# Recording a three-part product as three operations, and letting the scheduler place a wide product between two transposes

## The chip, the core and the metric

The kernel runs on one core of a Trainium2 chip. The metric is the device time of one execution in microseconds (us); the runs shown give the median of 3. The core's engines have queues of their own that run in order: TensorE (PE; its weight loads are a row of their own, PEld), VectorE (DVE), ScalarE (ACT), GpSimd (POOL), SyncE (SP, which issues transfers). A row of the trace names engine, source line, operation, and "written<-read" tiles by kind: s in SBUF, p and a in PSUM, m small tiles.

## The reference

Two decoder layers on 512 tokens of width 1024. Each mixes tokens by two attentions on one input projection (one with an index that selects 128 keys, one "stick-breaking"), gates and merges them, and then runs a mixture of 16 experts of which each token uses two. Cut to what matters:

```python
for l in range(DEPTH):
    proj = x @ w_in[l]                        # q, k, v, index, gates
    y_a = dsa_attention(...)                  # top-k by an indexer, softmax
    y_b = stick_breaking_attention(...)       # sigmoid, reversed cumulative product
    merged = g_a * (y_a @ w_branch_a) + g_b * (y_b @ w_branch_b)
    x = layer_norm(DN_ALPHA * x + merged @ w_out, ...)
    for e in range(N_EXPERTS):                # of the tokens whose combine[:, e] is not 0
        h = silu(xf @ exp_w_gate[e]) * (xf @ exp_w_up[e])
        y = y + combine[:, e:e + 1] * (h @ exp_w_down[e])
    x = layer_norm(DN_ALPHA * x + y, ...)
```

## The kernel before

**Products.** To keep float32 accuracy at the speed of the rounded type `float32r`, both factors are split into a high and a low part (`Chip.split`: a cast on ACT at L484, a subtraction on DVE at L495), and a product is three matmuls into one PSUM tile: low x high, high x low, high x high. `Chip.mm3` makes them. Most have a 128x128 stationary operand and 512 columns; I call one such matmul a wide product. There are about 5000 of them.

**Transposes.** Where a result has to be turned, PE transposes 128x128 pieces through the identity (`Chip.tr`, L445): 888 times. In the attentions they turn the probabilities of one head (1 to 4 pieces each), in the experts the gathered tokens (8 pieces for an expert, `prep`) and the hidden layer (4 pieces, `down`, function `turn`). I call them turns, as the change does.

**Order of the work.** The kernel is not written in the order in which it runs. Every call records an `Op` with an engine, an assumed duration and the buffers that it reads and writes. `Recorder.plan` then plays a list scheduler: at each step it takes the engine that is free first, and of the operations that are ready there the one with the lowest `prio` (the place in which it was recorded, moved by `bump`). A planned start sets nothing but the order: the instructions are issued engine by engine in that order, and the chip runs each queue in order, with semaphores between engines. What is planned too early therefore waits at the head of its queue, and holds what stands behind it. In the plan a turn takes 0.11 us, and a three-part product is one operation, so nothing can stand between its matmuls:

```python
        if transpose is not None:
            dur = 0.11
...
    def mm3(self, out, lh, ll, rh, rl, start, stop):
        return self.mm(out, [(ll, rh), (lh, rl), (lh, rh)], start, stop)
```

**Stages.** Per layer: projections, indexer, both attentions and the gates woven together (80 to 365 us in the first layer, 800 to 1130 in the second); the output projection and the router (to about 440 and 1205); the 16 experts (to about 745 and 1500); the second norm. An expert needs 6.3 MB of weights, read by SP in 512 KB pieces. The tokens of an expert are fetched by an indirect transfer that POOL issues (`gather`, L1179) into a tile that `prep` turns. That fetch also claims the two `xh` tiles into which the turned tokens are split, and these exist for three experts, so the fetch for expert e waits until PE has read the tokens of expert e-3 for the last time. Result rows are scattered by POOL at L1185. The first expert takes its tokens from PSUM, without a fetch.

Of the kernel before, what the change touches and what calls it, by code (L numbers as in the profile page):

```python
# [11 lines left out]
F = mybir.dt.float32  # L12
FR = mybir.dt.float32r
# [15 lines left out]
NE = 16  # L29
# [56 lines left out]

class Op:
    __slots__ = ("eng", "dur", "fn", "deps", "prio", "allocs", "bufs", "succ", "wait", "ready", "start", "end", "nbytes",
                 "table", "n", "load", "cnt", "cols")


class Recorder:
# [3 lines left out]
    LAT = 0.14  # L96

    def __init__(self, nc, tc):
        self.nc, self.tc, self.ops, self.bump, self.after = nc, tc, [], 0, None
        self.plain = bacc.Bacc("TRN2", target_bir_lowering=False, num_devices=1)  # L100
        self.shapes, self.masks, self.tokens = {}, {}, {}

# [19 lines left out]
            self.masks[key] = (m if p0 < 64 else 0) | ((m << 64) if p0 + n > 64 else 0)  # L122
        return self.masks[key]

    def add(self, eng, dur, fn, writes=(), reads=(), wtok=(), rtok=(), nbytes=0, table=None, allocs=(), load=None):
        o = Op()
        o.eng, o.dur, o.fn, o.nbytes, o.table = eng, dur, fn, nbytes, table
        o.prio = len(self.ops) - self.bump
        o.deps, o.allocs, o.succ, o.n = set(), [], [], len(self.ops)
        bufs = {}  # L130
        for vs, wr in ((reads, False), (writes, True)):
            for v in vs:
                if not isinstance(v, View):
                    continue
                b, m = v.buf, self.mask(v)
                if not b.hist and b.slot is None:
                    assert wr, "read before any write"
                for m2, w2, o2 in b.hist:
                    if (wr or w2) and m & m2:
                        o.deps.add(o2)  # L140
                bufs[b] = 1
        for vs, wr in ((reads, False), (writes, True)):
            for v in vs:
                if isinstance(v, View):
                    b, m = v.buf, self.mask(v)
                    if b.first is None:
                        b.first = (o.prio, o.n)
                    if wr:
                        b.hist = [h for h in b.hist if h[0] & ~m or h[2] is o]
                    b.hist.append((m, wr, o))  # L150
        for v in allocs:
            bufs[v.buf] = 1
            if v.buf.first is None:
                v.buf.first = (o.prio, o.n)
        for toks, wr in ((rtok, False), (wtok, True)):
            for t in toks:
                h = self.tokens.setdefault(t, [])
                for w2, o2 in h:
                    if (wr or w2) and o2 is not o:
                        o.deps.add(o2)  # L160
                if wr:
# [12 lines left out]

    def plan(self):
# [6 lines left out]
        ready = {e: [] for e in engs}  # L182
        barrier = []
        dma_free, hw_free = 0.0, 0.0
        table = None
        left = {}
        frees = []
        for o in self.ops:
# [96 lines left out]
        while done < len(self.ops):  # L285
# [16 lines left out]
            else:  # L302
# [7 lines left out]
                if e == "ACT" and table is not None:  # L310
                    keep = [x for x in ready[e] if x[2].table in (None, table)]
                    if keep:
                        x = min(keep)
                        if x[0] < ready[e][0][0] + 400:
                            ready[e].remove(x)
                            heapq.heapify(ready[e])
                            o = x[2]
                if o is None:
                    o = heapq.heappop(ready[e])[2]
                o.allocs = [b for b in o.bufs if b.slot is None]  # L320
# [39 lines left out]
            else:  # L360
                if e == "ACT" and o.table is not None and o.table != table:
                    table = o.table
                    dur += 1.3
                if e == "PE":
                    if busy.get(int(t / TICK) - 1, 0) < COLUMNS:
                        dur *= 2
                    k = int((t + dur) / TICK)
# [52 lines left out]
class Chip:  # L420
# [10 lines left out]
    def psum(*vs):  # L431
        return 0.06 if any(isinstance(v, View) and v.buf.kind in "pa" for v in vs) else 0.0

    def mm(self, out, terms, start, stop, transpose=None, also=()):
        dt = {F: 4, FR: 1, BF: 1}
        n = self.n(out)
        if transpose is not None:
            dur = 0.11
        else:
            dur = sum(max(dt[x.dtype if not isinstance(x, View) else x.ap.dtype] * n, 256) / 2400 + 0.004 for _, x in terms)  # L440

        def fn():
            o = real(out)
# [5 lines left out]
        o = self.r.add("PE", dur, fn, [out], reads, allocs=also)  # L449
        o.cols = sum(n * w.shape[0] / P for w, _ in terms) + n * (transpose is not None)  # L450
        o.cnt = sum(2 if (x.ap.dtype if isinstance(x, View) else x.dtype) == F else 1 for _, x in terms) + (transpose is not None)
        return o

    def mm3(self, out, lh, ll, rh, rl, start, stop):
        return self.mm(out, [(ll, rh), (lh, rl), (lh, rh)], start, stop)

    def mm_side(self, outs, terms, stop, also=()):

# [77 lines left out]
THROTTLE = 3  # L536
CAP0, CAP1, CAP2 = 12, 19, 29
BUMP, KEEP, LATE, NXT = 50, 1, 0, 3


QUOTA = {"raw": 3, "w": 6, "wi": 10, "wo": 12, "ew": 24, "at": 2, "pt": 6, "xg": 2, "xh": 6, "x": 46}
# [2 lines left out]
def build(tc, x0, xT0, w_idx, w_main, w_br, w_out, w_exp, bgate, idxg, idxb,  # L544
          ln1g, ln1b, ln2g, ln2b, wrt, rbias, ln1c, hconst, tab0, out):
    nc = tc.nc
    with ExitStack() as ctx:
# [703 lines left out]
        def moe(l, tb, gi, gl, mci, loads, xacc, until, routed):  # L1251
# [24 lines left out]
            def gate_up(e, xhl, between=None):  # L1276
                xh, xl = xhl
                for i in (0, 2):
# [4 lines left out]
                    for c in parts:  # L1283
                        for kk in range(KD):
# [1 line left out]
                                w += weights(e, i + kk // 4)  # L1286
                            o = C.mm3(ps[:, c], xh[:, kk, :], xl[:, kk, :], w[kk][0][:, c], w[kk][1][:, c], kk == 0, kk == KD - 1)
                            if done is not None:
                                o.deps.add(done)
                        done = o  # L1290
                        if i:
                            C.tt(sg[:, c], sg[:, c], ps[:, c], OP.mult)
# [318 lines left out]
```

## Time and profile before

| | |
|---|---|
| median of 3 runs | 1542.97 us (1541.4 to 1545.42) |
| the profiled execution | 1544.22 us, span 1542.5 us |
| mean granted clock of PE | 0.985 of 2.4 GHz |
| PE busy | 1477.8 us (96%) |
| DVE busy | 1268.0 us (82%) |
| ACT busy | 896.6 us (58%) |
| DMA | 313 MB; 325 GB/s in the experts' stages |

Busy time of PE is the union of its matmul rows, whose ends are modelled. What a matmul takes away from the next is read from the distance of two starts instead. The profiled execution is 1.25 us longer than the median of the runs; 1.7 us of it lie outside the span.

### The profile page before, as it was taken

What the parts mean: (1) busy time and instruction counts of PE and PEld (TensorE: products, weight loads), DVE (VectorE), ACT (ScalarE), POOL (GpSimd) and SP (SyncE); (2) the same over time, 40 slices, a digit from 0 to 9 for tenths busy, and PEclk for the clock granted to TensorE, in tenths of its full rate; (3) what the DMA queues carried; (4) which work ended last, traced back from release to release, by engine and by line L of the source; (5) the groups of instructions that cost most, each with busy time, mean ns of one, the idle gap of its engine ahead of it and who ended that gap; (6) DMA issues with size and microseconds to landing.
All of it is one profiled execution on the core that took longest, in us unless ns stands there. A gap on an engine that the chain in (4) does not pass through costs nothing. (4 is left out here: it accounts for less than half of the span.)

```text
span 1542.5 us, 21103 instructions
## 1 busy us (share of the span) xinstructions
PE 1477.8 (96%) x7188; PEld 1177.3 (76%) x7188; DVE 1268.0 (82%) x2321; ACT 896.6 (58%) x1459; POOL 128.4 (8%) x131
## 2 busy tenths in 40 slices
PE   8999999999989999999799999999999899999985
PEld 7877777777867788888487777777778578877874
DVE  5699995877687999989875999867766889899987
ACT  4335543674147888888433455346841578878773
POOL 0000000000131211111010000000001311111100
PEclk9999999999999999999899999999999899999998
DMA  7222113118778899999712211221287789999993
GB/s 222 72 84 67 57 55 96 56 42 304 268 249 307 328 349 343 335 337 332 297 69 67 85 55 55 83 82 55 68 316 254 260 309 337 347 331 323 351 328 147
DMA packets 92708, 313.15 MB, mean 203 GB/s; under 512 B 15757, under 2 KB 15885, under 8 KB 92592
## 3 DMA queue, kind: packets, MB, share of 16 engines
q1 hardware_dynamic: 83152, 294.88, 54.6%
q0 software_dynamic: 9440, 16.83, 3.0%
q8 instruction: 60, 0.98, 0.3%
q14 instruction: 56, 0.46, 0.1%
HBM read 302.19 MB, written 25.31 MB: 212 GB/s over the span
## 5 line engine op out<-in xcount | busy, mean ns | idle before, releaser
L447 PE MATMUL p<-s,s 128*128 128x512 f32 (+1 forms) x5192 | 1267.1, 397 | 30.0 <-DVE s L495 25.0
L447 PEld LDWEIGHTS p<-s,s 128*128 128x128 f32 x5192 | 950.2, 190 | 240.2 <-DVE s L495 25.6
L495 DVE TENSOR_TENSOR s<-s,s 128x1024 fp32r<-128x1024 f32 (+3 forms) x534 | 621.2, 1196 | 140.2 <-ACT s L484 106.8
L484 ACT CAST s<-s 128x1024 fp32r<-128x1024 f32 (+2 forms) x526 | 515.7, 1030 | 200.9 <-PE p L447 130.6
L495 DVE TENSOR_TENSOR s<-a,s 128x256 fp32r<-128x256 f32 (+3 forms) x386 | 168.8, 480 | 43.9 <-ACT s L484 40.4
L484 ACT CAST s<-a 128x256 fp32r<-128x256 f32 (+2 forms) x354 | 126.2, 414 | 123.7 <-PE a L445 107.1
L445 PE MATMUL a<-ident,s 128*128 128x128 f32 x888 | 132.3, 277 | 12.4 <-DMA s<-x1d,m 7.1
L445 PEld LDWEIGHTS a<-ident,s 128*128 128x128 f32 x888 | 106.2, 142 | 43.6 <-DVE s L495 11.4
L523 POOL TENSOR_TENSOR m<-m,nhalf 128x1 f32<-128x1 f32 x24 | 17.8, 743 | 902.1 <-DVE m L495 902.1
L480 ACT ACTIVATE s<-a 128x512 f32<-128x512 f32 (+3 forms) x156 | 61.8, 450 | 47.1 <-PE a L447 28.0
L484 ACT COPY s<-a 64x512 f32<-64x512 f32 (+1 forms) x48 | 27.8, 583 | 97.2 <-PE a L445 45.9
L487 ACT ACTIVATE s<-p,m 128x512 f32<-128x512 f32 (+1 forms) x64 | 44.2, 690 | 53.5 <-PE p L447 49.3
L464 PE MATMUL a<-s,s 64*128 64x384 f32 (+3 forms) x456 | 67.4, 351 | 0.0
L1179 POOL DMA_INDIRECT s<-x1d,m x30 | 42.9, 1430 | 265.6 <-PE p L447 248.3
L1185 POOL DMA_INDIRECT yd<-s,m x32 | 46.1, 1440 | 209.6 <-ACT s L487 189.6
L447 PEld LDWEIGHTS a<-s,s 128*128 128x128 f32 x360 | 57.1, 188 | 7.8 <-issue 2.4
L447 PE MATMUL a<-s,s 128*128 128x324 f32 (+4 forms) x360 | 62.4, 321 | 0.2
L464 PEld LDWEIGHTS a<-s,s 64*128 64x128 f32 x456 | 41.3, 185 | 27.6 <-issue 20.0
L495 DVE MAX8 m<-s 128x8 f32<-128x256 f32 (+2 forms) x96 | 53.5, 557 | 1.8
L495 DVE MATCH_REPLACE8 s<-m,s 128x256 f32<-128x256 f32 (+2 forms) x96 | 52.1, 543 | 0.0
L495 DVE TENSOR_TENSOR_SCAN s<-s 128x128 f32<-128x128 f32 (+3 forms) x64 | 51.1, 814 | 0.1
L484 ACT CAST s<-p 128x512 fp32r<-128x512 f32 x48 | 27.9, 588 | 35.6 <-DVE p L495 19.8
(108 smaller groups left out, 650.6 us busy)
## 6 DMA issues: line engine op xcount, KB each, us to landing
s<-in_w_exp SPq DMA_DIRECT2D x384, 512.0 KB
s<-in_w_main SPq DMA_DIRECT2D x79, 512.0 KB
s<-in_w_br SPq DMA_DIRECT2D x16, 512.0 KB
s<-in_w_out SPq DMA_DIRECT2D x16, 512.0 KB
s<-yd SPq DMA_DIRECT2D x16, 512.0 KB
x1d<-s SPq DMA_DIRECT2D x8, 512.0 KB
s<-x1d SPq DMA_DIRECT2D x8, 512.0 KB
s<-in_w_idx SPq DMA_DIRECT2D x8, 324.0 KB
```

The source lines that it names most:

```text
L445: self.nc.tensor.transpose(o, real(transpose[0]), transpose[1])
L447: self.nc.tensor.matmul(o, real(w), real(x), start=start and i == 0, stop=stop and i == len(terms) - 1)
L464: self.nc.tensor.matmul(real(o), real(t[i][0]), real(t[i][1]), start=i == 0, stop=stop and i == len(t) - 1)
L480: self.nc.scalar.activation(real(out), real(src), func, bias=real(bias), scale=real(scale), **kw)
L484: return self.r.add("ACT", 0.1 + self.psum(out, src) + self.n(out) * 0.833e-3, lambda: self.nc.scalar.copy(real(out), real(src)), [out], [ ...
L487: return self.r.add("ACT", 0.2 + self.n(out) * 0.833e-3, lambda: self.nc.scalar.mul(real(out), real(src), real(c)), [out], [src, c])
L495: getattr(self.nc.vector, method)(real(out), *[real(a) for a in args], **{k: real(x) for k, x in kw.items()}, **({} if accum is None else ...
L523: return self.r.add("POOL", 0.47, lambda: self.nc.gpsimd.tensor_tensor(real(out), real(a), e, OP.pow), [out], [a])
L1179: R.add("POOL", 1.04, lambda: nc.gpsimd.indirect_dma_start(out=real(dst), out_offset=None, in_=x1d, in_offset=IOA(ap=real(idx), axis=0), * ...
L1185: s_ = nc.gpsimd.indirect_dma_start(out=yd, out_offset=IOA(ap=real(idx), axis=0), in_=real(src), in_offset=None, bounds_check=2 * S - 1, o ...
```

## The change

Three edits. `mm3` records its three matmuls as three operations; the first two are marked `more`, so that the count from which `prio` is taken (`tick`) goes on only once per product. Operations on PE get a `form`: "turn" for a transpose or a narrow float32 product, "wide" for a `float32r` product with 256 columns or more. And in `plan`, when the last operation on PE was a turn and the next by priority is a turn too, the first ready wide one whose `prio` is less than 1000 behind is taken ahead of it. A turn that follows something other than a turn is planned 0.075 us shorter. In the experts' `gate_up` the order between the two halves of the last product now binds all three operations.

```diff
@@ class Recorder: add
-        o.prio = len(self.ops) - self.bump
+        o.prio, o.form = self.tick - self.bump, form
+        self.tick += not more
...
@@ plan
+                if e == "PE" and form == "turn" and ready[e][0][2].form == "turn":
+                    for x in sorted(x for x in ready[e] if x[2].form == "wide" and x[0] < ready[e][0][0] + NEAR):
+                        x[2].allocs = [b for b in x[2].bufs if b.slot is None]
+                        if x[2].allocs:
...
+                            w = room(x[2], t)
+                            if w is None or w > t + 1e-9:
+                                continue
+                        ready[e].remove(x)
+                        heapq.heapify(ready[e])
+                        o = x[2]
+                        break
...
                 if e == "PE":
+                    if o.form == "turn" and form != "turn":
+                        dur -= 0.075
+                    form = o.form
...
@@ class Chip: mm
+        form = None
+        if transpose is not None or n <= 2 * NE and kinds == [F]:
+            form = "turn"
+        elif n >= 256 and kinds[0] == FR:
+            form = "wide"
...
     def mm3(self, out, lh, ll, rh, rl, start, stop):
-        return self.mm(out, [(ll, rh), (lh, rl), (lh, rh)], start, stop)
+        self.mm(out, [(ll, rh)], start, False, more=True)
+        self.mm(out, [(lh, rl)], False, False, more=True)
+        return self.mm(out, [(lh, rh)], False, stop)
...
+NEAR = 1000
...
@@ gate_up
                             if done is not None:
-                                o.deps.add(done)
+                                for x in R.ops[-3:]:
+                                    x.deps.add(done)
```

The same matmuls are issued, 888 turns and all products among them. What moves is their order, and with it the order on the other engines. Counted over the whole program, 698 turns were followed directly by a turn and 180 are now; of the 518 pairs that are parted, 174 lie in the experts (85 and 89 in the two layers), 344 elsewhere. Turns that stand alone between two other matmuls go from 28 to 654.

**Place 1: PE in an attention of the first layer.** Two heads' probabilities (s_2918 before, s_2831 after, three pieces each, into two PSUM tiles a) are turned beside a projection into four p tiles. Before:

```order
L445 MATMUL a_2971<-ident,s_2918 128x128 x3
L447 MATMUL p_2658<-s_195,s_2696 128x512
L447 MATMUL p_2658<-s_212,s_2663 128x512
L447 MATMUL p_2658<-s_195,s_2663 128x512
L447 MATMUL p_2675<-s_195,s_2696 128x512
L447 MATMUL p_2675<-s_212,s_2663 128x512
L447 MATMUL p_2675<-s_195,s_2663 128x512
L445 MATMUL a_2992<-ident,s_2918 128x128 x3
L447 MATMUL p_2692<-s_195,s_2696 128x512
L447 MATMUL p_2692<-s_212,s_2663 128x512
L447 MATMUL p_2692<-s_195,s_2663 128x512
```

The turns stand in two runs of three, and whole three-part products between the runs. Now, the same turns on the same engine:

```order
L463 MATMUL a_2911<-ident,s_2831 128x128
L465 MATMUL p_2861<-s_137,s_2733 128x512
L463 MATMUL a_2911<-ident,s_2831 128x128
L465 MATMUL p_2861<-s_139,s_2700 128x512
L463 MATMUL a_2911<-ident,s_2831 128x128
L465 MATMUL p_2861<-s_137,s_2700 128x512
L463 MATMUL a_2925<-ident,s_2831 128x128
L465 MATMUL p_2889<-s_137,s_2733 128x512
L463 MATMUL a_2925<-ident,s_2831 128x128
L465 MATMUL p_2889<-s_139,s_2700 128x512
L463 MATMUL a_2925<-ident,s_2831 128x128
```

Each run of three turns is opened, and one matmul of a three-part product (into p_2861, then p_2889) stands behind each turn.

**Place 2: PE in the first layer's experts.** Before, the hidden layer of an expert (s_5780) and the tokens of expert 9 (s_5674, eight pieces) are turned in one run of twelve, between the gate product of expert 8 (p_5902) and its up product (p_5980):

```order
L447 MATMUL p_5902<-s_5924,s_5492 128x512
L447 MATMUL p_5902<-s_5914,s_5492 128x512
L447 MATMUL p_5902<-s_5914,s_5493 128x512
L447 MATMUL p_5902<-s_5924,s_5492 128x512
L447 MATMUL p_5902<-s_5914,s_5492 128x512
L445 MATMUL a_5955<-ident,s_5780 128x128 x4
L445 MATMUL a_5966<-ident,s_5674 128x128 x4
L445 MATMUL a_5971<-ident,s_5674 128x128 x4
L447 MATMUL p_5980<-s_5922,s_5493 128x512
L447 MATMUL p_5980<-s_5936,s_5492 128x512
L447 MATMUL p_5980<-s_5922,s_5492 128x512
```

Nothing stands between the twelve. Now the same pattern is found one expert later, for the tokens of expert 10 (s_5865) and the gate and up products of expert 9 (p_6083, p_6138):

```order
L465 MATMUL p_6083<-s_6105,s_5679 128x512
L465 MATMUL p_6083<-s_6093,s_5679 128x512
L463 MATMUL a_6136<-ident,s_5979 128x128
L465 MATMUL p_6138<-s_6102,s_5680 128x512
L463 MATMUL a_6136<-ident,s_5979 128x128
L465 MATMUL p_6138<-s_6116,s_5679 128x512
L463 MATMUL a_6136<-ident,s_5979 128x128
L465 MATMUL p_6138<-s_6102,s_5679 128x512
L463 MATMUL a_6136<-ident,s_5979 128x128
L465 MATMUL p_6138<-s_6102,s_5680 128x512
L463 MATMUL a_6154<-ident,s_5865 128x128
L465 MATMUL p_6138<-s_6116,s_5679 128x512
```

The run of twelve has become twelve single turns, with eleven wide products between them.

**Place 3: PE at the tokens of expert 9, now.** The activations of expert 6 (s_5122 high, s_5123 low) are read for the last time in the fifth row of this piece; from there on the fetch for expert 9 may start:

```order
L465 MATMUL p_5604<-s_5651,s_5122 128x512
L465 MATMUL p_5604<-s_5634,s_5122 128x512
L465 MATMUL p_5604<-s_5634,s_5123 128x512
L465 MATMUL p_5604<-s_5651,s_5122 128x512
L465 MATMUL p_5604<-s_5634,s_5122 128x512
L465 MATMUL p_5664<-s_5660,s_5510 128x512
L465 MATMUL p_5664<-s_5642,s_5510 128x512 x2
L465 MATMUL p_5664<-s_5660,s_5510 128x512
L465 MATMUL p_5664<-s_5642,s_5510 128x512
```

The rows after the fifth already belong to the down product of expert 5 (p_5664). Further on the first turn of the tokens of expert 9 (s_5678) stands here, in the fourth row, between two matmuls of the gate product of expert 7 (p_5735):

```order
L465 MATMUL p_5699<-s_5671,s_5510 128x512
L465 MATMUL p_5735<-s_5713,s_5304 128x512
L463 MATMUL a_5609<-ident,s_5479 128x128
L463 MATMUL a_5739<-ident,s_5678 128x128
L465 MATMUL p_5735<-s_5724,s_5303 128x512
L465 MATMUL p_5735<-s_5713,s_5303 128x512
L465 MATMUL p_5735<-s_5713,s_5304 128x512
L465 MATMUL p_5735<-s_5724,s_5303 128x512
L465 MATMUL p_5735<-s_5713,s_5303 128x512
```

Between the last reading and this turn stand 24 wide products and 5 turns. Before, the tokens of expert 9 were turned behind the gate product of expert 8 (place 2), 120 wide products and 16 turns after the same point. Now the distance is also short for expert 4 (24 products, 4 turns) and expert 14 (30, 5) of the first layer, and for expert 5 (19, 12), expert 10 (24, 5) and expert 15 (30, 5) of the second; for every other expert from the fourth on it is 37 products or more, and before it was 66 or more for all.

## Rows read from the trace of the kernel before

**Rows 1.** The page: busy time of PE, and its two large groups.
```profile
PE 1477.8 (96%) x7188; PEld 1177.3 (76%) x7188; DVE 1268.0 (82%) x2321; ACT 896.6 (58%) x1459; POOL 128.4 (8%) x131
...
L447 PE MATMUL p<-s,s 128*128 128x512 f32 (+1 forms) x5192 | 1267.1, 397 | 30.0 <-DVE s L495 25.0
...
L445 PE MATMUL a<-ident,s 128*128 128x128 f32 x888 | 132.3, 277 | 12.4 <-DMA s<-x1d,m 7.1
```

**Rows 2.** Windows: stretch, length, busy of PE, PEld, DVE, ACT, POOL, clock, DMA.
```profile
80.00:365.00 285.00, 283.15 (x1442) 219.86 (x1440) 240.16 (x546) 151.99 (x341) 0.00 (x0) 1.00 0.23 74
...
440.00:745.00 305.00, 292.01 (x1377) 238.01 (x1376) 272.38 (x290) 244.10 (x293) 52.83 (x39) 0.99 0.91 325
...
800.00:1130.00 330.00, 328.31 (x1659) 256.54 (x1657) 262.45 (x606) 165.51 (x362) 1.19 (x2) 1.00 0.22 71
...
1205.00:1500.00 295.00, 283.48 (x1307) 230.21 (x1305) 260.91 (x277) 233.61 (x280) 47.16 (x39) 0.99 0.92 325
```

**Rows 3.** Waits of PE in all: total, times, longest.
```profile
PE p L447 <- DVE s L495: 31.1, 27, 6.8
PE a L445 <- DMA s<-x1d,m: 7.1, 3, 2.7
```

**Rows 4.** Timeline, attention: start, length, engine, line, operation, count; single turns.
```profile
297.61 0.14 PEld L445 LDWEIGHTS a<-ident,s 128*128 128x128 f32 x1
297.84 0.27 PE L445 MATMUL a<-ident,s 128*128 128x128 f32 x1
297.84 0.54 PEld L447 LDWEIGHTS p<-s,s 128*128 128x128 f32 x3
297.87 0.94 PE L447 MATMUL p<-s,s 128*128 128x512 f32 x3
...
298.65 0.27 PE L445 MATMUL a<-ident,s 128*128 128x128 f32 x1
```

**Rows 5.** Timeline of PE, experts: fifteen wide products and the next turn.
```profile
1479.67 3.56 PE L447 MATMUL p<-s,s 128*128 128x512 f32 x15
1483.07 0.60 PE L445 MATMUL a<-ident,s 128*128 128x128 f32 x4
```

**Rows 6.** Timeline of PE, experts: runs of twelve turns.
```profile
563.38 1.47 PE L445 MATMUL a<-ident,s 128*128 128x128 f32 x12
564.61 16.62 PE L447 MATMUL p<-s,s 128*128 128x512 f32 x72
581.07 1.47 PE L445 MATMUL a<-ident,s 128*128 128x128 f32 x12
```

**Rows 7.** Timeline of PE, attention: a run of four.
```profile
907.40 0.60 PE L445 MATMUL a<-ident,s 128*128 128x128 f32 x4
907.76 2.31 PE L447 MATMUL p<-s,s 128*128 128x512 f32 x9
909.91 1.37 PE L447 MATMUL a<-s,s 128*128 128x512 f32 x8
```

**Rows 8.** Timeline of POOL: the fetch in the cycle of rows 6; line L1179's landing.
```profile
570.62 1.49 POOL L1179 DMA_INDIRECT s<-x1d,m  x1 [10.29 <-PE p L447]
...
DMA to landing us min/median/max: 4.5/7.2/9.1
```

**Rows 9.** Timeline of PE at the ends of both expert stages: last weights.
```profile
733.11 0.98 PE L447 MATMUL p<-s,s 128*128 128x256 f32 x6 [0.97 <-DVE s L495]
...
735.96 1.21 PE L447 MATMUL p<-s,s 128*128 128x256 f32 x8 [0.74 <-DVE s L495]
737.68 2.78 PE L447 MATMUL p<-s,s 128*128 128x256 f32 x21 [0.51 <-DVE s L495]
...
1501.86 4.95 PE L447 MATMUL p<-s,s 128*128 128x256 f32 x27 [4.53 <-PEq L1203]
```

More of the change, by code (lines that the diff above doesn't have):

```diff
@@ L88 @@
     __slots__ = ("eng", "dur", "fn", "deps", "prio", "allocs", "bufs", "succ", "wait", "ready", "start", "end", "nbytes",
-                 "table", "n", "load", "cnt", "cols")
+                 "table", "n", "load", "cnt", "cols", "form")
 class Recorder:
@@ L98, in __init__ @@
     def __init__(self, nc, tc):
-        self.nc, self.tc, self.ops, self.bump, self.after = nc, tc, [], 0, None
+        self.nc, self.tc, self.ops, self.bump, self.after, self.tick = nc, tc, [], 0, None, 0
         self.plain = bacc.Bacc("TRN2", target_bir_lowering=False, num_devices=1)
@@ L123, in mask, with add @@
         return self.masks[key]
-    def add(self, eng, dur, fn, writes=(), reads=(), wtok=(), rtok=(), nbytes=0, table=None, allocs=(), load=None):
+    def add(self, eng, dur, fn, writes=(), reads=(), wtok=(), rtok=(), nbytes=0, table=None, allocs=(), load=None, form=None, more=False):
         o = Op()
         o.eng, o.dur, o.fn, o.nbytes, o.table = eng, dur, fn, nbytes, table
-        o.prio = len(self.ops) - self.bump
+        o.prio, o.form = self.tick - self.bump, form
+        self.tick += not more
         o.deps, o.allocs, o.succ, o.n = set(), [], [], len(self.ops)
@@ L184, in plan @@
         dma_free, hw_free = 0.0, 0.0
-        table = None
+        table, form = None, None
         left = {}
@@ L317, in plan @@
                             o = x[2]
+                if e == "PE" and form == "turn" and ready[e][0][2].form == "turn":
+                    for x in sorted(x for x in ready[e] if x[2].form == "wide" and x[0] < ready[e][0][0] + NEAR):
+                        x[2].allocs = [b for b in x[2].bufs if b.slot is None]
+                        if x[2].allocs:
+                            for s in slots.values():
+                                s.sort()
+                            w = room(x[2], t)
[5 more added lines that the diff above has]
+                        break
                 if o is None:
@@ L432, in psum, with mm @@
         return 0.06 if any(isinstance(v, View) and v.buf.kind in "pa" for v in vs) else 0.0
-    def mm(self, out, terms, start, stop, transpose=None, also=()):
+    def mm(self, out, terms, start, stop, transpose=None, also=(), more=False):
         dt = {F: 4, FR: 1, BF: 1}
@@ L439, in mm @@
         else:
-            dur = sum(max(dt[x.dtype if not isinstance(x, View) else x.ap.dtype] * n, 256) / 2400 + 0.004 for _, x in terms)
+            kinds = [x.dtype if not isinstance(x, View) else x.ap.dtype for _, x in terms]
+            dur = sum(max(dt[k] * n, 256) / 2400 + 0.004 for k in kinds)
         def fn():
@@ L448, in mm @@
         reads = [x for t in terms for x in t] + ([transpose[0]] if transpose else [])
-        o = self.r.add("PE", dur, fn, [out], reads, allocs=also)
+        form = None
[3 more added lines that the diff above has]
+            form = "wide"
+        o = self.r.add("PE", dur, fn, [out], reads, allocs=also, form=form, more=more)
         o.cols = sum(n * w.shape[0] / P for w, _ in terms) + n * (transpose is not None)
```

## The prediction

> **What bounds the kernel now.** I read the page first, then busy time by stage, then single starts on PE. The page shows PE busy for 96% of the span, nearly all of it in the wide products and the turns [rows 1]. The windows show where that is a bound: in the two attention stretches PE is busy for 283.15 of 285 us and 328.31 of 330, at full clock [rows 2]. The waits of PE over the whole run come to about 40 us, 31.1 on DVE and 7.1 on the fetch of tokens [rows 3]; hardly any lie in the attentions. So there each 10 ns that a matmul takes more or less moves the end. In the expert stages PE is busy for 292 of 305 and 283 of 295 us, while the DMA engines are at 0.91 and 0.92 [rows 2]: two bounds close together, and at the end of both stages PE waits for the last weights, 0.97 + 0.74 + 0.51 = 2.2 us in the first layer and 4.5 in the second [rows 9].
>
> **What a turn costs, and whether a wide product beside it makes it cheaper.** The change takes a turn behind a wide product for 0.035 us instead of 0.11. The starts seem to say so: a turn starts at 297.84 and the wide product behind it at 297.87 [rows 4]. But a row of a matmul can start while it still waits for its weights. The better measure is a whole period. Fifteen wide products take 1483.07 - 1479.67 = 3.40 us, 0.2267 each [rows 5]. In the attention, from one single turn to the next (one turn and three wide products) 298.65 - 297.84 = 0.81 us pass; less 3 x 0.2267 = 0.68 that leaves **0.13 for a turn that stands alone** [rows 4]. In a run of twelve, 564.61 - 563.38 = 1.23 us hold eleven steps from turn to turn and the 0.03 to the first wide product: **0.109 for a turn in a run** [rows 6]. A run of four with nine wide products takes 909.91 - 907.40 = 2.51, less 2.04 that is 0.47, or 0.118 each [rows 7]: between the two, as it should be. The rows say why: the weight load of the wide product begins at 297.84, with the turn and not before it [rows 4], so nothing hides it; a turn is over sooner than the load of the next weights, whatever matmul these belong to. The wide product hides the load of the turn behind it, but a load was not what the turn lacked: it is what the turn fails to cover for its successor.
>
> The Trainium skill has a rule that speaks against the change in the same way: its page "TensorE: Matmul & The Clock Gate", section "LDWEIGHTS (loading the stationary operand)", makes a load cost its 128 columns over 1.2 GHz, some 107 ns, whichever matmul uses it. By that rule the sum of this term is nil; the rows agree with 0.109, and add a little for each parted run.
>
> **The sum.** Parted pairs cost 0.13 - 0.109 = 0.021 each, with rows rounded to 0.01, so 0.01 to 0.03. I take 0.015, since in rows 4 two wide products follow on the one behind the turn and carry some of that, and between two single turns now mostly one stands.
> - Outside the experts: 344 x 0.015 = **5.2 us** (3.4 to 10), on the path, since PE has no idle time there [rows 2].
> - In the experts: 174 x 0.015 = 2.6 us.
> - Fetches met too early. In the cycle of rows 6 the run of turns is followed by 24 wide products that read an expert's tokens for the last time; they end at 564.61 + 0.09 + 24 x 0.2267 = 570.14, and POOL starts the next fetch at 570.62 [rows 6, 8], 0.5 later. It lands 4.5 to 9.1 us after that, 7.2 in the median [rows 8]. So the tokens can be turned 7.7 us after the last reading (5.0 to 9.6). At 0.2267 for a wide product and 0.12 for a turn PE now comes there after 5.9 and 6.0 us (24 products and 4 or 5 turns: experts 4 and 9 of the first layer, 10 of the second), 5.8 (19 and 12: expert 5 of the second) and 7.4 (30 and 5: experts 14 and 15). That makes waits of 1.8 + 1.7 + 1.7 + 1.9 + 0.3 + 0.3 = **7.7 us**, between nothing and 19. The queue is in order, so the gate products behind the first turn wait too. Before, PE came there after 120 products and 16 turns, 29 us, and waited for a fetch three times in all, 7.1 us [rows 3].
> - What the experts' stages give back: if the weights come no later than now, a PE that is behind finds them landed, and the 2.2 and 4.5 us at the ends [rows 9] shrink. Each layer adds more than that (1.3 + 3.8 and 1.3 + 3.9), so I take off all 6.7; if the loads wait for tiles that PE frees, nothing is taken off.
> - The rest of the order: ACT and DVE get the turned tile later, since four turns with wide products between them take 4 x 0.35 us instead of 0.44, and a PSUM tile is held as much longer. PE has other work meanwhile. I take 0, with 5 us to either side.
>
> Sum: 5.2 + 2.6 + 7.7 - 6.7 = 8.8 us on the profiled execution's 1544.2, which is 1.25 above the median of the runs; from the median 1542.97 that is **1552 us**.
>
> **Rivals.**
> - *The wide product does hide the turn.* Then each parted pair saves 0.109 - 0.034 = 0.075, as the change assumes: 344 x 0.075 = 25.8 us outside the experts; the 13 us inside are lost to the weights, which PE waits for already. Time about 1517. For it: the starts 0.03 apart. Against it: the period of 0.81 and the load that begins with the turn [rows 4]. On the same page, section "Architectural detail: the array is 16× 32×32, not 1× 128×128", the skill says that PE's queue can pull a weight load ahead of matmuls in flight; if it pulled it past a turn, this rival would hold. The trace shows it ahead of one matmul, not of two. 6%.
> - *No change to be measured.* The parted pairs cost 0.01, the fetches land in 5 us, and what is left in the experts goes into the waits for weights: 344 x 0.01 = 3.4 us, 1546. For it: the 4.5 us minimum [rows 8] and the end of the second layer's experts [rows 9]. Against it: a median of 7.2, and PE without idle time in the attentions. 27%.
> - *Faster through the finer grain.* A product recorded whole cannot be opened for something urgent, and is planned only once all its parts are ready. PE waits 27 times for DVE, 31.1 us [rows 3]. If each of these were shorter by the two matmuls that can now go ahead, 27 x 0.45 = 12 us would go, and if the fetches then cost nothing net: 1543 - 12 + 5.2 = 1536. It decides once more than 10 us of those waits are gone. Against it: the semaphores were held by each matmul alone already, so on the chip the first of a product never waited for what only the second reads; only the order can gain. 10%.
>
> **How the numbers follow.** The forecast, with its own range 1547 to 1563, gets 57%. What a measurement can tell from no change is 0.3%, 4.6 us, so slower begins at 1547.6. Faster has the first and the third rival, 16%; the same, 27%; slower, 57%. The range goes from 1536, the third rival, to 1565, where five of the six fetches land near their latest or the weights absorb nothing; that leaves out the first rival and a part of the extremes.
>
> **What would show it.** In the profile of the changed kernel: a single turn and the wide product behind it start 0.03 apart, but a period of one turn and one wide product takes 0.34 to 0.36 us (0.26 if the first rival holds). The union of the turns' busy time rises from 132 to over 200 us, without any turn costing that much, since their rows of 0.27 us no longer overlap; the mean of a wide product's row rises by about 0.01 us for the same reason. PE's waits for the fetched tokens rise from 7.1 us to 12 or more, with the new ones at experts 9 and 14 of the first layer and 10 and 15 of the second. The waits at the ends of the expert stages get shorter. The attention stretches get longer by 2 to 3 us each. I am wrong if the attentions get shorter, or if PE's waits for DVE fall by more than 10 us.

## The result, and the profile after

The changed kernel takes 1615.28 us in the median (1612.79 to 1620.53), the kernel before in the same runs 1544.11: ratio 1.0461, 95% interval 1.0434 to 1.0488. It is slower by 71 us; 1552 were predicted, with a range up to 1565.

The page of the changed kernel (L463 was L445, L465 was L447, L509 was L484, L520 was L495, L1205 was L1179), beside [rows 1]:
```profile
PE 1513.2 (93%) x7188; PEld 1176.7 (73%) x7188; DVE 1268.5 (78%) x2321; ACT 903.0 (56%) x1455; POOL 120.5 (7%) x131
...
L465 PE MATMUL p<-s,s 128*128 128x512 f32 (+1 forms) x5192 | 1351.3, 410 | 42.8 <-DVE s L520 29.7
...
L463 PE MATMUL a<-ident,s 128*128 128x128 f32 x888 | 221.9, 283 | 37.1 <-DMA s<-x1d,m 18.4
```
The turns' busy time (132.3 before) and the mean of a wide product's row (397 before) rise because rows no longer overlap. The idle time in front of the turns has tripled, from 12.4 us. The mean granted clock is 0.973 (0.985 before): with its two levels, 1.2 and 2.4 GHz, that is some 87 us at the lower one, against 46.

The same stages in windows (stretch, length, busy PE, PEld, DVE, ACT, POOL, clock, DMA), beside [rows 2]:
```profile
80.00:376.00 296.00, 287.63 (x1431) 215.38 (x1431) 240.28 (x542) 153.00 (x337) 0.00 (x0) 1.00 0.24 80
459.00:786.00 327.00, 305.68 (x1377) 243.34 (x1376) 276.07 (x291) 249.14 (x298) 46.08 (x39) 0.95 0.87 307
842.00:1186.00 344.00, 335.63 (x1660) 254.17 (x1658) 264.07 (x606) 166.64 (x359) 1.34 (x2) 1.00 0.23 78
1270.00:1575.00 305.00, 285.89 (x1317) 228.40 (x1314) 261.39 (x267) 239.60 (x285) 45.02 (x37) 0.98 0.88 311
```
All four stretches hold the work of before, within 11 matmuls. The attentions are 11 and 14 us longer, with 8 us of idle time in each where there were under 2. The experts are 22 and 10 us longer, at a granted clock of 0.95 and 0.98, and with a smaller share of the DMA engines.

The waits of PE over the run, beside [rows 3]:
```profile
PE p L465 <- DVE s L520: 34.0, 26, 6.7
PE a L463 <- DMA s<-x1d,m: 18.4, 7, 3.4
PE a L463 <- ACT s L509: 15.4, 63, 1.0
...
PE p L465 <- ACT s L509: 5.0, 4, 3.7
```
The third line is new. Before, turns waited for ACT once:
```profile
PE a L445 <- ACT s L484: 0.5, 1, 0.5
```
Of the 63 waits, 56 lie in the two attentions. PE there (start, length, operation, idle time before):
```profile
242.71 0.27 PE L463 MATMUL a<-ident,s 128*128 128x128 f32 x1
242.74 0.48 PE L465 MATMUL p<-s,s 128*128 128x512 f32 x1
243.44 0.33 PE L463 MATMUL a<-ident,s 128*128 128x128 f32 x1 [0.23 <-ACT s L509]
243.53 0.48 PE L465 MATMUL p<-s,s 128*128 128x512 f32 x1
243.84 0.27 PE L463 MATMUL a<-ident,s 128*128 128x128 f32 x1
243.87 0.48 PE L465 MATMUL p<-s,s 128*128 128x512 f32 x1
244.19 0.27 PE L463 MATMUL a<-ident,s 128*128 128x128 f32 x1
244.21 0.48 PE L465 MATMUL p<-s,s 128*128 128x512 f32 x1
244.92 0.33 PE L463 MATMUL a<-ident,s 128*128 128x128 f32 x1 [0.23 <-ACT s L509]
```
and ACT beside it, with the weight load of the turn at 243.44:
```profile
243.44 0.14 PEld L463 LDWEIGHTS a<-ident,s 128*128 128x128 f32 x1 [0.54 <-ACT s L509]
...
243.02 0.37 ACT L509 CAST s<-a 128x256 fp32r<-128x256 f32 x1 [0.62 <-PE a L463]
243.81 0.27 ACT L509 CAST s<-a 128x128 fp32r<-128x128 f32 x1 [0.42 <-PE a L463]
244.49 0.37 ACT L509 CAST s<-a 128x256 fp32r<-128x256 f32 x1 [0.42 <-PE a L463]
```
From turn to turn 0.35 us pass (243.84 to 244.19), or 0.73 where the later one is the third of its tile (242.71 to 243.44). `transpose_p` copies the first two pieces of a tile with one operation and the rest with another. With a wide product between the turns, the plan puts the first copy ahead of the third turn, and the third turn then has to wait for it: ACT reads from 243.02 to 243.39, the turn starts at 243.44. In all 63 waits it starts 0.05 us after the end of a copy, and in 61 of them 0.73 or 0.74 us after the turn before, with one matmul between: 63 x 0.38 us make 24 us, by this estimate.

It is the program that holds the turn. In the program as built, 31 turns of the first layer wait, by a semaphore, for ACT's copy of other columns of their own tile; before it was 1, since nearly all turns of a tile went before its copy. The planner follows what depends on what by columns, so it does not know of this wait. What the chip would do without the semaphore, no run here shows.

A fetch that is met too early, on PE, and the end of the first layer's experts (beside [rows 9]):
```profile
501.51 3.00 PE L465 MATMUL p<-s,s 128*128 128x512 f32 x12
507.84 1.11 PE L463 MATMUL a<-ident,s 128*128 128x128 f32 x4 [3.33 <-DMA s<-x1d,m]
...
768.66 0.38 PE L465 MATMUL p<-s,s 128*128 128x256 f32 x1 [3.69 <-ACT s L509]
769.92 2.75 PE L465 MATMUL p<-s,s 128*128 128x256 f32 x11 [0.87 <-DVE s L520]
772.99 0.58 PE L465 MATMUL p<-s,s 128*128 128x256 f32 x1 [0.32 <-ACT s L509]
774.25 2.71 PE L465 MATMUL p<-s,s 128*128 128x256 f32 x11 [0.68 <-DVE s L520]
777.47 4.21 PE L465 MATMUL p<-s,s 128*128 128x256 f32 x18 [0.51 <-DVE s L520]
...
1576.71 4.61 PE L465 MATMUL p<-s,s 128*128 128x256 f32 x20 [6.11 <-PEq L1229]
```
The last line is the end of the second layer's experts (PEq is PE's sequencer). The fetch on POOL, and on ACT the cast of weights that came late:
```profile
498.84 1.46 POOL L1205 DMA_INDIRECT s<-x1d,m  x1 [13.19 <-DMA s<-in_w_exp]
...
768.84 1.05 ACT L509 CAST s<-s 128x1024 fp32r<-128x1024 f32 x1 [0.24 <-DMA s<-in_w_exp]
```
and windows around both places:
```profile
505.00:512.00 7.00, 4.16 (x14) 3.47 (x15) 1.79 (x2) 1.60 (x3) 1.51 (x1) 0.63 0.87 336
...
764.00:770.00 6.00, 1.44 (x10) 0.99 (x8) 4.60 (x6) 4.67 (x5) 0.00 (x0) 0.97 1.00 365
770.00:777.00 7.00, 5.97 (x23) 5.08 (x23) 4.85 (x4) 4.40 (x5) 0.00 (x0) 0.50 1.03 416
777.00:784.00 7.00, 5.32 (x22) 4.52 (x22) 4.40 (x5) 3.09 (x4) 0.00 (x0) 0.50 0.57 217
```
The turn at 507.84 comes 9.0 us after POOL began the fetch, 3.3 of them idle, and the clock of the stretch is 0.63. At 770 to 784 it is 0.50, the lower level (1.2 GHz), behind an idle time of 3.7 us and with shorter ones in it. So a wait there costs its own length and then the slower matmuls behind it.

### The profile page after: what moved, and what is told of

It reads as the page before. It is cut to its first block, busy times and chain, and to the rows that moved or that the text cites. A ratio compares the mean times of both kernels' runs of the same rounds, so it can differ in the third digit from the quotient of the medians.

```text
span 1618.5 us, 21103 instructions
## 1 busy us (share of the span) xinstructions
PE 1513.2 (93%) x7188; PEld 1176.7 (73%) x7188; DVE 1268.5 (78%) x2321; ACT 903.0 (56%) x1455; POOL 120.5 (7%) x131
## 5 line engine op out<-in xcount | busy, mean ns | idle before, releaser
L465 PE MATMUL p<-s,s 128*128 128x512 f32 (+1 forms) x5192 | 1351.3, 410 | 42.8 <-DVE s L520 29.7
L465 PEld LDWEIGHTS p<-s,s 128*128 128x128 f32 x5192 | 966.6, 193 | 277.8 <-DVE s L520 38.9
L520 DVE TENSOR_TENSOR s<-s,s 128x1024 fp32r<-128x1024 f32 (+2 forms) x534 | 622.9, 1194 | 159.5 <-ACT s L509 98.4
L509 ACT CAST s<-s 128x1024 fp32r<-128x1024 f32 (+1 forms) x526 | 521.9, 1030 | 220.1 <-PE p L465 153.9
L463 PE MATMUL a<-ident,s 128*128 128x128 f32 x888 | 221.9, 283 | 37.1 <-DMA s<-x1d,m 18.4
L509 ACT CAST s<-a 128x256 fp32r<-128x256 f32 (+2 forms) x354 | 140.5, 408 | 202.2 <-PE a L463 195.1
L520 DVE TENSOR_TENSOR s<-a,s 128x256 fp32r<-128x256 f32 (+3 forms) x386 | 176.6, 480 | 75.8 <-ACT s L509 63.1
L463 PEld LDWEIGHTS a<-ident,s 128*128 128x128 f32 x888 | 122.0, 143 | 82.5 <-ACT s L509 38.3
L509 ACT COPY s<-a 64x512 f32<-64x512 f32 (+1 forms) x48 | 28.0, 583 | 102.2 <-PE a L463 32.9
L465 PE MATMUL a<-s,s 128*128 128x324 f32 (+4 forms) x360 | 66.3, 325 | 0.8 <-DVE s L520 0.8
L465 PEld LDWEIGHTS a<-s,s 128*128 128x128 f32 x360 | 57.3, 190 | 7.8 <-DVE s L520 1.4
L1205 POOL DMA_INDIRECT s<-x1d,m x30 | 37.5, 1251 | 284.8 <-PE p L465 261.3
L520 DVE MAX8 m<-s 128x8 f32<-128x384 f32 (+2 forms) x96 | 53.1, 555 | 1.8
L520 DVE MATCH_REPLACE8 s<-m,s 128x256 f32<-128x256 f32 (+2 forms) x96 | 52.1, 542 | 0.0
L520 DVE TENSOR_TENSOR_SCAN s<-s 128x128 f32<-128x128 f32 (+3 forms) x64 | 51.5, 815 | 0.5
L520 DVE TENSOR_TENSOR s<-s 128x127 f32<-128x127 f32 (+5 forms) x96 | 45.5, 484 | 0.6
```

What stands on the lines that cost most here:

```text
L463: self.nc.tensor.transpose(o, real(transpose[0]), transpose[1])
L509: return self.r.add("ACT", 0.1 + self.psum(out, src) + self.n(out) * 0.833e-3, lambda: self.nc.scalar.copy(real(out), real(src)), [out], [ ...
L520: getattr(self.nc.vector, method)(real(out), *[real(a) for a in args], **{k: real(x) for k, x in kw.items()}, **({} if accum is None else ...
L1205: R.add("POOL", 1.04, lambda: nc.gpsimd.indirect_dma_start(out=real(dst), out_offset=None, in_=x1d, in_offset=IOA(ap=real(idx), axis=0), * ...
```

## The experiments

To see where each kernel loses, I gave every matmul one price (the lower quartile of the start-to-start times of its kind over all kernels) and asked when each kernel had done the same sum of work. How many us each stands behind the kernel before, at equal work (e_split_only and e_split_att, whose orders are the same through the first layer's attention, differ there by up to 2 us):
```
work  before at  changed  split_only  split_sj  sticky  whole_copy  nie_late_copy  whole_products  whole_sb
 150    185.5      2.6       3.7        1.1     -1.3      -1.5         -2.6           -3.0          -4.5
 250    311.0     17.5       7.4        1.3      1.0       3.8          2.7            0.5           0.9
 300    374.0     14.9       4.4        1.3     12.6       7.3          6.3           30.1           0.9
 350    426.7     17.2       8.1        1.3     19.0      10.2          9.1           33.5           0.9
 600    713.9     31.0       8.7       -0.3     38.7      21.7         15.9           45.3           2.3
 700    846.3     42.2      16.8       -0.0     43.2      34.0         24.3           52.0           3.1
 850   1032.7     57.5      24.8        0.4     43.4      36.2         26.6           55.6           3.7
 950   1157.5     61.6      28.3        1.8     43.4      43.7         35.7           84.7           3.7
1050   1284.6     66.8      31.0       -3.6     38.0      44.9         38.1           87.2           3.3
1250   1507.9     72.6      30.4       -4.4     39.1      54.1         37.4           89.6           3.2
```
The first layer's attention lies at 150 to 350, its experts at 350 to 650; the second's from 750 and from 1000 on. The changed kernel loses 15 us in each attention (work 150 to 250 and 700 to 850), 25 in the first layer's experts (350 to 700) and, from 1050 on, 6 in the second's. In the runs below the lines of the helpers shift a little (turns L463 or L468, ACT's casts L507 to L516).

### The recording in three operations

**e_split_only**
```
-                if e == "PE" and form == "turn" and ready[e][0][2].form == "turn":
+                if False:
-                        dur -= 0.075
+                        dur -= 0.0
```


> Products recorded as three operations, but the rule that puts a wide product between two turns taken out, and the 0.075 us off a turn's price with it. Theory (the loss is made by the order that the rule writes: third turns that wait for ACT's copy of their own tile in the attentions, and fetches met too early in the experts): the recording alone costs nearly nothing, 1545 us (1537 to 1555), turns' idle time before ACT's L509 under 2 us as in the kernel before. Rival 1 (the finer recording itself moves the work): 1575 us or more.


1571.88 us, ratio 1.0146 (1.0122 to 1.017). Turns hardly wait for ACT (4.0 us in all rows, those of matmuls and of weight loads; under 2 were expected, 53.7 stand in the changed kernel), but the recording alone, with the order that it leads to, costs a third of the loss. Rival 1 has its effect, if not its size; my theory of "nearly nothing" falls.

**e_split_joined** (e_split_only, and in `mm3`, with a, b, o the three thirds):
```
+        a.deps.update((b.deps | o.deps) - {a, b})
```


> Products recorded as three operations without the rule, as in e_split_only (1571.88 us, 1.0146), but the first third may start only when everything that the whole product reads is there. Theory (the 24 us come from first thirds that start early and hold TensorE and a bank for operands that are late): 1552 us (1545 to 1560). Rival (they come from what is put between the thirds, and from the planner's greedy order as such: its own plan is 13 us longer for e_split_only and 19 us for this one): 1572 to 1580 us.


1573.74 us, 1.0158 (1.0113 to 1.0203): the early start alone is not it.

**e_split_att** (e_split_only with `mm3` whole in `moe`)


> Products recorded as three operations outside the expert stages only, whole inside, without the rule. Theory (of the 24 us of e_split_only 8 arise in each attention, the rest at the last expert of layer 0 and in the router): the loss at the last expert of layer 0, 8 us, goes, the rest stays: 1564 us (1557 to 1571). Rival (the last expert is late for the order at which its weights were loaded before): 1572 us within 5.


1578.9 us, 1.0206 (1.0168 to 1.0244). Neither held. The loss does not belong to where the products are split. With whole products in them the first layer's experts lose 18 us (work 350 to 650), where e_split_only loses 9; two waits of 4.65 and 4.32 us stand there. The order planned behind the first attention changes with the edit.

**e_split_sticky** (in place of the rule and the lower price)
```
+                if e == "PE" and last is not None and last.more:
+                    for x in [x for x in ready[e] if x[2].n == last.n + 1]:
+                        ready[e].remove(x); heapq.heapify(ready[e]); o = x[2]
```


> As e_split_only, but a product's next third goes right behind the last where it is ready; first thirds may still start before the operands of the others are there. Theory (the 24 us come from what parts the thirds, since e_split_joined, which took the early start away and kept the parting, took 1573.74 us): the attentions end within 3 us of before, and only the fetches of layer 0, which the plan meets 7.2 us after their issue from expert 6 on, cost some 20 us with their half clock: 1565 us (1555 to 1575), of which under 5 us in layer 1. Rival (the early start costs in the attentions too): 1580 us.


1584.85 us, 1.0234 (1.0199 to 1.0268): the rival's figure, with a part of the theory in it. The first layer's attention now loses at its end (1.0 at 250, 19.0 at 350; the plan itself is 12 us late there). Its experts, whose fetches the plan meets 7.2 us after their issue, lose 20 (19.0 to 38.7), and the second layer nothing. Turns of several experts wait for their fetch:
```profile
531.46 0.52 PE L468 MATMUL a<-ident,s 128*128 128x128 f32 x3 [1.24 <-DMA s<-x1d,m]
551.52 0.41 PE L468 MATMUL a<-ident,s 128*128 128x128 f32 x2 [0.67 <-DMA s<-x1d,m]
591.48 0.41 PE L468 MATMUL a<-ident,s 128*128 128x128 f32 x2 [1.88 <-DMA s<-x1d,m]
```

**e_split_sj** (the edits of e_split_joined and e_split_sticky)


> Products recorded as three operations without the rule, but the planner gives TensorE the next third of a product right behind the last one, and the first third waits for all that the product reads: the record is finer, the order nearly the one of before (its plan ends at 1422, as before's). Theory (the 24 us of e_split_only are what comes between and ahead of the thirds): 1545 us (1538 to 1552). Rival (the finer record moves the banks' and tiles' release or the other queues' waits by itself): 1560 us or more.


1543.32 us, 0.9987 (0.9965 to 1.0009). The finer record costs nothing. What it lets the planner do, start a first third early or put other work between thirds, costs 24 us; one of the two alone is enough.

### The third turn and ACT's copy

**e_whole_copy** (in `transpose_p`)
```
+            end = R.ops[-1]
-            C.split(ah[:, :n, ts], al[:, :n, ts], p3[:, :n, :])
+            C.split(ah[:, :n, ts], al[:, :n, ts], p3[:, :n, :]).deps.add(end)
```


> The changed kernel, in which the first copy out of a tile of turned pieces in the attentions has to come behind the last turn of that tile, in the plan and so in the order. Theory: the third turns wait for no copy of their own tile any more; the idle time of turns that ACT's L509 ends falls from 53.7 us in all rows to under 25, and the time by 20 to 30 us, half clock behind the waits with it: 1590 us (1583 to 1598). Rivals 2 and 3: no change, 1615 us within 5.


1602.96 us, 1.0355 (1.0317 to 1.0393). All rows' idle time before ACT in turns falls from 53.7 to 21.1 us, and those parts of the attentions lose 5 and 2 us where the changed kernel loses 15 and 15 (work 150 to 250 and 700 to 850). The turns' idle time before ACT, in the changed kernel and here (us, times), and PE's waits here:
```profile
ACT s L509: 53.7, 135
...
ACT s L509: 21.1, 48
...
PE a L463 <- DMA s<-x1d,m: 17.6, 8, 3.7
PE a L463 <- ACT s L509: 6.2, 23, 1.0
```
The mechanism is shown, but the time is outside the range: 12 us are gained by the medians, where 20 to 30 were expected. The edit reaches the probabilities' tiles alone. Other tiles, such as the turned queries and keys, are copied out in two parts as well, and 23 of the 63 waits stay; the 40 that go are worth 40 x 0.38 = 15 us. Against that, other waits come in at the attentions' ends and in the second layer's experts.

**e_whole_products** (`mm3` whole, the rule and the lower price kept)


> The rule and the lower price kept, the products recorded whole as before. Theory (the recording costs 24 us by itself and the rule comes on top): third turns still wait for ACT's copy (71 turns wait for ACT alone in the order, 73 in the changed kernel), and some fetches are met early: 1591 us (1581 to 1601). Rival (the loss needs rule and recording together, a third of a product between two turns): 1565 us or less.


1637.01 us, 1.0599 (1.0543 to 1.0654): worse than the changed kernel, which neither theory allowed. Third turns stand behind a copy in its order too, but three wide matmuls between two turns hide it. PE, first in the attention, then at its end:
```profile
211.18 0.27 PE L463 MATMUL a<-ident,s 128*128 128x128 f32 x1
211.21 0.94 PE L465 MATMUL p<-s,s 128*128 128x512 f32 x3
211.99 0.27 PE L463 MATMUL a<-ident,s 128*128 128x128 f32 x1
212.01 0.94 PE L465 MATMUL p<-s,s 128*128 128x512 f32 x3
212.79 0.27 PE L463 MATMUL a<-ident,s 128*128 128x128 f32 x1
...
350.44 0.44 PE L463 MATMUL a<-ident,s 128*128 128x128 f32 x2 [3.99 <-DVE s L518]
...
356.06 2.15 PE L463 MATMUL a<-ident,s 128*128 128x128 f32 x8 [2.49 <-DVE s L518]
...
375.12 1.49 PE L465 MATMUL p<-s,s 128*128 128x512 f32 x3 [2.73 <-DVE s L518]
```
ACT and the windows there:
```profile
211.49 0.37 ACT L507 CAST s<-a 128x256 fp32r<-128x256 f32 x1 [0.59 <-PE a L463]
```
```profile
344.00:358.00 14.00, 7.42 (x38) 4.84 (x36) 7.72 (x27) 9.83 (x26) 0.00 (x0) 0.77 0.00 1
358.00:376.00 18.00, 12.55 (x56) 8.95 (x56) 13.91 (x49) 11.51 (x32) 0.00 (x0) 0.69 0.00 0
```
The period stays 0.81 us over the copy at 211.49, and up to 250 us of work nothing is lost. Then 30 us go at the end of each attention: the wide products have been spent between turns, and when the last heads need something to put beside DVE's softmax, none is left. From 345.5 to 375.1 us PE runs no product into a p tile; it waits up to 4 us, at 0.77 and 0.69 of the clock. The planner saw this coming: its plan ends at 1444, 21 us later than before's.

**e_whole_sb** (as e_whole_products, but turns have a form in `sb_heads` only)


> Products whole, and the rule with its lower price for the turns of the first kind of heads only (sb_heads), nowhere else. Theory (e_whole_products lost its time where the wide products had run out, at the end of the second kind of heads, and in the experts; three wide matmuls between two turns hide ACT's copy, one does not): 1546 us (1538 to 1554), no waits of turns for ACT above 5 us in all. Rival (breaking a run of turns costs in itself): 1560 us or more.


1546.04 us, 1.0006 (0.999 to 1.0022), as expected; turns wait for ACT 7.8 us in all rows (5 were given as the most), 0.5 of them on PE. 90 pairs of turns are parted (698 to 608). At the predicted 0.015 us each that would be 1.4 us, which the interval cannot tell from nothing. So parting runs costs next to nothing where the stock of wide products lasts, and wins nothing.

### The experts and their fetches

**e_no_discount**
```
-                        dur -= 0.075
+                        dur -= 0.0
```


> The changed kernel with a turn after a wide product planned at its full 0.11 us, the rule kept. Theory: the planner's clock for TensorE runs less ahead of the chip, so fetches are met later and the experts win back about 15 us, while the third turns of the attentions wait as before (74 turns wait for ACT alone in the order, 73 in the changed kernel): 1600 us (1590 to 1610). Rival 2 (the false price is the whole cause): 1550 us. Rival 3 (a turn between wide products costs by itself, wherever it stands): 1615 us, within 4.


1595.49 us, 1.0296 (1.0269 to 1.0322): in the theory's range. The experts win back 15 us as expected, but in one layer alone. The first layer's experts lose about as much as in the changed kernel (22 us against 25, work 350 to 650): its plan meets the fetches from expert 6 on 7.2 us after their issue. It is the second layer's that won (work 1000 to 1250). The price of 0.035 us, that the chip does not honour, is thus a cause of its own: 1.65 of the 4.61% go with it.

**e_not_in_experts** (no form for turns recorded by `moe`)


> The changed kernel with the rule and the lower price applied everywhere but in the two expert stages (their turns have no form). Theory: what the attentions and the router lost stays (about 36 us over both layers), what the experts lost (some 35 us) goes: 1580 us (1572 to 1590), and the expert stages last as long as in the kernel before within 5 us each. Rival 3 (a cost of each parted pair): of the 226 pairs of turns that the change parts 190 stay parted, so 60 of the 71 us stay, 1604 us.


1603.44 us, 1.0341 (1.0293 to 1.039). The theory falls: without the rule in them, the first layer's experts still lose over 20 us. The time is the figure of rival 3, and the rule's absence does not refute it: the twelve turns of an expert stand apart here all the same, for the most part as 4, 2, 2, 1 and 3 (129 pairs are left of 202 at work 350 to 660). Against a cost of each pair speaks its size in the trace: at 0.015 us the 73 pairs make 1 us. The plan of this kernel again meets these fetches after 7.2 us. So the loss in this stage does not need the rule in it; whether the cycle into which the plan falls makes it is tested next. It is not the only way to lose there: e_split_att lost 18 us with the fetches met as late as before, 27.7 us after their issue.

**e_nie_late** (e_not_in_experts, and in the planner)
```
-                o.end = dma_free + 0.9
+                o.end = dma_free + (4.9 if any(b.group == "xg" for b in o.bufs) else 0.9)
```


> The kernel without the rule in the expert stages, and with the planner's landing of a gather 4 us later. In the plan, the time from a gather's issue to the first turn of its tile in layer 0 was 7.2 us from expert 6 to 15 and is 27.7 us now. Theory (fetches met too early): the row of waits of 0.6 to 1.4 us per expert in layer 0 goes, the experts of layer 0 get some 20 us shorter, 1603.44 us become 1582 us (1574 to 1590). Rival (the stream of weights): 1600 us within 5.


1595.24 us, 1.0331 (1.0278 to 1.0384). In its profile the first layer's experts lose 5 us where they lost 22 (work 350 to 600), which is what was expected of the cycle. The twelve turns stand together again with it (184 of the 202 pairs). In the medians the 8 us are within the intervals. Unclear.

**e_late_copy** (the changed kernel with this line and e_whole_copy's)


> The changed kernel with two things mended: the first copy out of a tile of turned pieces comes behind the tile's last turn, and the planner takes a gathered tile of rows to land 4 us later than it did. Theory (what the recording alone does not explain is third turns that wait for ACT's copy, plus turns that meet their fetch too early): 1602.96 us of the copy mended alone fall by the turns' waits for a fetch and some half clock behind them, to 1587 us (1580 to 1595). Rival (the experts are late because the stream of weights is, and the wait for a fetch only covers that): 1600 us or more.


1589.75 us, 1.0296 (1.024 to 1.0353), in the range. Turns wait for fetches 6.5 us instead of 17.6, but the wide products behind DVE's weights wait 45.1 instead of 37.6, so most of it comes back as another wait:
```profile
PE p L465 <- DVE s L520: 45.1, 33, 6.9
PE a L463 <- DMA s<-x1d,m: 6.5, 5, 2.5
```

**e_nie_late_copy** (all three)


> The changed kernel with the rule off in the expert stages, the first copy behind the last turn of its tile, and a gather planned to land 4 us later. Theory (what is left is what the recording alone costs): 1577 us (1570 to 1584). Rival (the rule costs as such where it stands): 1590 us or more.


1581.31 us, 1.0228 (1.0193 to 1.0262), in the range. But the ratio lies above that of e_split_only by more than the intervals, so what is left is not the recording alone.

**b_late_fetch** (the kernel before with the later landing)


> The kernel before, with the planner's landing of a gather 4 us later and nothing else. Theory: the three waits of turns for a fetch (7.1 us in all) go, and some half clock behind them: 1541 us (1534 to 1547). Rival: TensorE has nothing else to do there, and the waits become others: 1547 us within 4.


1550.39 us, 1.0037 (1.0009 to 1.0064): the rival. Turns wait 3.9 us for fetches instead of 7.1, but products wait 8.0 us for PE's sequencer instead of 4.5. Later fetches gain nothing by themselves.

No version beats the kernel before.

## Why the prediction was wrong

- **A turn's price: right.** 0.13 us for a turn alone was read from [rows 4]; the period of one turn and one wide product is 0.35 (0.34 to 0.36 predicted), which leaves 0.12 for the turn, near the 0.109 + 0.015 of the sum. Around 211 us in e_whole_products one turn and three wide products take 0.81 again. The wide product does not hide the turn, and parting a run costs too little to be seen (e_whole_sb).
- **"ACT and DVE get the turned tile later ... I take 0, with 5 us to either side": this step failed.** It reckoned with tiles that are held longer, while "PE has other work meanwhile". But PE's queue is in order, and the third turn itself has to wait for a copy out of its own tile. A mechanism was missing, worth 0.38 us in 63 turns, 24 us by estimate; putting 40 of them right won 12 us. The Trainium skill has a rule that such a wait follows: "PSUM — Partial Sum Buffer", section "PSUM bank collisions raise a hardware error", tells kernel authors to guard PSUM with semaphores "by **bank × quadrant** (by bank is the simple version), not by address". The trace agrees with such a guard: the third turn starts 0.05 us after the copy of the other columns ends. I had not weighed that page.
- **The split was not priced.** The sum had no term for the recording; the third rival saw only a gain in it. The order that it allows costs 24 us without the rule; the finer record itself costs nothing (e_split_sj). PE's waits for DVE did not shrink: 34.0 us [rows 3: 31.1].
- **Fetches met too early: waits about right, the price too small.** New waits stand at experts 4 and 9 of the first layer, 5, 10 and 15 of the second, 12.2 us against the 7.7 of the sum; at expert 14 of the first there is none. The 18.4 us in all (12 or more predicted) hold 6.2 at the first experts, where waits stood before. The term left out what follows each: matmuls at the lower clock (0.63 in the 7 us around 507.84).
- **"I take off all 6.7": the sign was wrong.** At the end of the first layer's experts the waits grew from 2.2 us [rows 9] to 3.69 + 0.87 + 0.32 + 0.68 + 0.51 = 6.1, and from 770 to 784 PE ran at 1.2 GHz; in the second layer the wait grew from 4.53 to 6.11. A PE that was late did not find its weights landed: in the first layer ACT's casts of them waited for transfers.
- **The attentions: wrong.** 2 to 3 us each were predicted; 11 and 14 were lost by the windows, 15 and 15 at equal work. Neither of the two signs named for being wrong came (shorter attentions, 10 us less waiting for DVE): both looked for a gain.

Of the 4.61% that the change costs, 1.46 come with the order that the split record allows, 1.06 go when the copy is put behind the last turn, and 0.6 and 0.7 more with later fetches and without the rule in the experts (the intervals of neighbours overlap in these two steps); 0.8 stay unassigned. The parts do not add freely: with the products whole, the rule costs 5.99%, and leaving out the lower price alone takes 1.65 off, which cuts across these parts. Why the finer order loses 24 us, wait by wait, stays open beyond this: the plan itself ends 13 us later (1435 against 1422), and by its mean clock, 0.974 over 1574.7 us, PE ran some 82 us at the lower level, 46 before.

## What to carry to other kernels

Before putting work between writes to one PSUM tile, see who reads that tile: here a copy of its first part, placed between, held the next write by a semaphore that the planner did not know. One matmul of 0.23 us beside a copy of 0.37 did not hide that, three did. Filler is a stock: spent where PE is busy anyway, it is missing where PE waits. A list scheduler that was promised 25 us (1422 to 1397) can lose 71, so ask what its prices leave out, and test finer recording and the new rule apart.

## What the hardware showed that I had not expected

- A turn that follows a copy of other columns of its own tile starts 0.05 us after the copy's end: 0.73 us from turn to turn instead of 0.35. The wait is a semaphore of the program; whether the chip would need it is not shown.
- After 3.3 and 3.7 us without a matmul, the granted clock was 0.63 in the 7 us that hold the wait's end, and 0.50 over the next 14. Here a wait of 3 us cost more than itself.
